# GpSimd's sums and gate products in the up-projection stage moved to VectorE

## The chip, the cores and the metric

The kernel runs on one core of one Trainium2 chip. The metric is the device time of one execution in microseconds (us). Three runs of the kernel before took 2186.55, 2191.22 and 2193.07 us; the median, 2191.22 us, is the time before.

## The reference

One block of a hybrid model, all in float32: 2048 tokens of width 1024, and a context of 256 tokens that gives only the starting state. What matters here is its second half, the feed-forward layer:

```
x = x + g1 * mix_x
x = x + g2 * swiglu(modulate(rmsnorm(x, norm2), sh2, sc2), w_up, w_down)
return rmsnorm(x, norm_f)

def swiglu(h, w_up, w_down):
    u = h @ w_up                      # 1024 -> 2 * 2816
    g, a = split(u, 2)
    return (silu(g) * a) @ w_down     # 2816 -> 1024
```

`g2` is a gate of 1024 numbers. Since it scales the columns of the layer's output, it can be multiplied into the columns of `w_down`.

## The kernel before

Every large product is done in two ways at once. First, a matrix is split into two halves in each direction, and seven products of half-size blocks, with sums of blocks as operands, stand in for eight (a scheme of Strassen's kind). Second, each float32 operand is split into a high and a low part, and each block product is three matmuls: high by high, high by low, low by high. ScalarE makes the high part (a cast, L146), VectorE the low part by subtraction (L149). A matmul has 128 rows and 512 columns.

The program has three long stages. From the start to about 840 us stand the projections, the scans of the mixer and the second norm. The **up-projection** runs from about 868 to 1760 us, in two halves of the tokens with 22 units each. The **down-projection** follows to the end. In the up-projection one unit is seven block products of 12 matmuls each (`product`, L586 to L588), 84 in all, which are named here by their right operand, h0 to h6, in program order. Their left operands come from two `raw` tiles of `w_up` (L633): the two for h0 and h1 are split as they are (`vt`), the others from block sums `ws` (L560) into `wh` and `wl`. The products h0, h2, h4 and h6 of a unit use one PSUM tile `pa`, h3 and h5 use `pg`, and h1 uses `pb`. Products h2, h4 and h6 add to what is in `pa`. After h4 VectorE reads `pa` into `a1` (L1266), and h6 may write `pa` only after that read. There are three `raw` buffers, and a unit needs two, so the loads for the next unit wait for the block sums of this one.

After every second unit `act_sums` forms four sums of blocks of the layer's activations (`small`, L1204) and stores seven blocks to HBM. In the second half of the tokens `w_sums` runs once per two units as well: it loads two 128x1024 tiles `big` of `w_down`, multiplies each half by the gate (L1230, four instructions), forms four differences (L1204) and stores seven blocks. The gate comes in a tile `adacc`. The sums go through four buffers `adaw`, each of which must have been stored before it is written again. At the start of the stage `last_norm` forms four differences (L1176). All of these, 180 instructions of 128x512, are on GpSimd (POOL).

The order on each engine is not the order of the text: a scheduler sets it from its own estimate of when each operand will be ready, and each engine then runs its list in that order. The loads and stores named here are issued by SyncE (SP), which also keeps to its list: a store whose source is not ready holds up the loads behind it.

Of the kernel before, what the change touches and what calls it, by code (L numbers as in the profile page):

```python
# [12 lines left out]
ALU = mybir.AluOpType  # L13
# [8 lines left out]
def tile_hybrid_block(ctx: ExitStack, tc: tile.TileContext, x, c, cx, c_ctx, w_ada, b_ada, norm1, w_in, conv_qk,  # L22
                      gate_bias, pool_w, pool_scale, head_norm, w_out, norm2, w_up, w_down, norm_f, out):
    nc = tc.nc
# [15 lines left out]
    def pool(name, bufs=1, side="left"):  # L40
        return tc.tile_pool(name=name, bufs=bufs, side=side, reuse_waits="tile")

    def psum(name, bufs):
        return tc.tile_pool(name=name, bufs=bufs, space=PSUM, reuse_waits="tile")
# [236 lines left out]
    def turn(psp, name, xs, d0, d1, a, b):  # L281

        for k0 in range(0, KD, 2):
            pt = psp.tile([P, 512], F32, name=name)
            for kk in range(2):
                for e in range(2):
                    o = kk * 256 + e * P
                    nc.tensor.transpose(out=pt[:, o:o + P], in_=xs[e][:, (k0 + kk) * P:(k0 + kk + 1) * P],
                                        identity=ident)
            for kk in range(2):  # L290
                k = k0 + kk
                src = pt[:, kk * 256:(kk + 1) * 256].rearrange("p (e c) -> p e c", e=2)
                dst = d0[:, :, k] if k < 4 else d1[:, :, k - 4]
                if kk:
                    nc.vector.tensor_scalar(dst, src, a[:, k:k + 1], b[:, k:k + 1], op0=ALU.mult, op1=ALU.add)
                else:
                    nc.scalar.activation(dst, src, AF.Identity, bias=b[:, k:k + 1], scale=a[:, k:k + 1])
            yield
# [58 lines left out]
    with pool("adap", 4, "right") as ap_:  # L357
        xc, turned = None, None
        for g in range(4):
# [39 lines left out]
            def col(o):  # L399
# [3 lines left out]
                                    op=ALU.add)  # L403
# [119 lines left out]
    def load_B(src, j, stp, name, bufs=3):  # L523

        t = b_tile(j)
        for k in range(4):
            st = stp.tile([P, 512], F32, name=name if isinstance(name, str) else name[k % 2], bufs=bufs)
            nc.scalar.dma_start(st, src[:, ORDER[j], k])
            split(st, t[:, 0, k], t[:, 1, k], nc.scalar, nc.vector)
        Btile[j] = t  # L530
# [94 lines left out]
    def load_raws(srcs, other=None):  # L625
        raws = []
        for src in srcs:
            if other is not None and raws:
                st = other.tile([P, KD, P], F32, name="rawx")
            else:  # L630
                st = rwp.tile([P, KD, P], F32, name="raw")
            with tc.issue_after(n_last.ins):
                raw_last[0] = nc.sync.dma_start(st, src.rearrange("(k p) c -> p k c", p=P))  # L633
            raws.append(st)
        return raws
# [141 lines left out]
    for half in range(2):  # L777
# [5 lines left out]
        if half == 0:  # L783
# [7 lines left out]
            def fin():  # L791
                fins.pop()(tp, "tp")
# [333 lines left out]
    def up_cols(f):  # L1126
        return [w_up[:, o + f * P:o + (f + 1) * P] for o in (0, DFF)]
# [35 lines left out]
    def last_norm(pair, xs):  # L1163

        half, i = divmod(pair, 4)
        yield
        d0 = last_x[0].rearrange("p (e k c) -> p e k c", e=2, k=4)
        d1 = xl.tile([P, 2, 4, P], F32, name="big")
        with tc.issue_after(mm_last[0].ins):
            for _ in turn(pmp, "pm", xs, d0, d1, A2, B2):  # L1170
                pass
        dst = s_hb[half][:, :, :, i * P:(i + 1) * P]

        def diff(a, b):
            t = adr.tile([P, 4, P], F32, name="adaw", bufs=4)
            nc.gpsimd.tensor_tensor(t, a, b, op=ALU.subtract)  # L1176
            return t
        t1 = diff(d0[:, 1], d0[:, 0])
        t2 = diff(d1[:, 1], t1)
        for b, t in ((0, d0[:, 0]), (1, d1[:, 0]), (2, d1[:, 1]), (3, t1), (4, t2), (5, diff(d1[:, 1], d0[:, 1])),  # L1180
                     (6, diff(d1[:, 0], t2))):
            nc.sync.dma_start(dst[:, b], t)
        yield
# [6 lines left out]
    with ExitStack() as pr:  # L1190
        wp = pr.enter_context(pool("m_w", 1))
        up_wp[0] = wp
        fin = None
        tmp = pr.enter_context(pool("m_a", 1))
        adr = pr.enter_context(pool("m_ad", 1))
        pup = pr.enter_context(psum("pup2", 2))

        def store(i, m, half, src):

            (nc.scalar if half and m == NM - 1 else nc.sync).dma_start(s_act[i, m, :, half], src)  # L1200

        def small(a, b, op):
            t = adr.tile([P, 512], F32, name="adaw", bufs=4)
            nc.gpsimd.tensor_tensor(t, a, b, op=op)  # L1204
            return t

        def act_sums(m, half, A11, A21, A12, A22):

            store(0, m, half, A11)
            store(1, m, half, A12)  # L1210
            store(6, m, half, A22)
            s1 = small(A21, A22, ALU.add)
            store(3, m, half, s1)
            s2 = small(s1, A11, ALU.subtract)
            store(4, m, half, s2)
            store(5, m, half, small(A11, A21, ALU.subtract))
            store(2, m, half, small(A12, s2, ALU.subtract))

        def w_sums(m):

            w1, w2 = (xl.tile([P, D], F32, name="big") for _ in range(2))
            with tc.issue_after(raw_last[0].ins):
                nc.sync.dma_start(w1, w_down[m * P:(m + 1) * P])
                nc.sync.dma_start(w2, w_down[(NM + m) * P:(NM + m + 1) * P])
            lo, hi = slice(0, 512), slice(512, 1024)
            for n in (lo, hi):
                g2r = adr.tile([P, 544], F32, name="adacc")[:, 0:512]
                nc.sync.dma_start(g2r, s_g[3:4, n].to_broadcast([P, 512]))
                for w in (w1, w2):
                    nc.gpsimd.tensor_tensor(w[:, n], w[:, n], g2r, op=ALU.mult)  # L1230
            nc.sync.dma_start(s_t[0, m], w1[:, lo])
            nc.sync.dma_start(s_t[1, m], w2[:, lo])
            nc.sync.dma_start(s_t[2, m], w2[:, hi])
            t1 = small(w1[:, hi], w1[:, lo], ALU.subtract)
            nc.sync.dma_start(s_t[3, m], t1)
            t2 = small(w2[:, hi], t1, ALU.subtract)
            nc.sync.dma_start(s_t[4, m], t2)
            nc.sync.dma_start(s_t[5, m], small(w2[:, hi], w1[:, hi], ALU.subtract))
            nc.sync.dma_start(s_t[6, m], small(w2[:, lo], t2, ALU.subtract))

        for half in range(2):
            if half:
                Btile = [None] * 7
            acts = []
            for ff in range(NF):
                m, fh = divmod(ff, 2)
                f = fh * NM + m
                first = half == 0 and f == 0
                make = up0 if first else operands(load_raws(up_cols(f)), up_wp)
                A = A0 if first else {}  # L1250
                for j, i in enumerate(ORDER):
                    if i not in A:
                        A[i] = make(i)
                    if Btile[j] is None:
                        load_B(s_hb[half], j, wp, "hst")
                g = [tmp.tile([P, 512], F32, name=f"g{n}", bufs=2) for n in range(2)]
                a1 = tmp.tile([P, 512], F32, name="a1")

                def sink(r, n, ps, sb):
                    if r == 0:  # L1260
                        nc.vector.tensor_tensor(g[n], ps, sb, op=ALU.add)  # L1261
                        nc.scalar.activation(g[n], g[n], AF.Silu)  # L1262
                        if n == 1:
                            nc.vector.tensor_tensor(g[1], g[1], a1, op=ALU.mult)  # L1264
                    elif n == 1:
                        nc.vector.tensor_tensor(a1, ps, sb, op=ALU.add)  # L1266
                    else:
                        nc.vector.tensor_tensor(g[0], g[0], ps, op=ALU.mult)
                norm = last_norm(order[-1] // 2, [X_.pop(m_) for m_ in (NCH - 1, NCH - 2)]) if first else iter(())
                for _ in unit(A, pup, tmp, sink):  # L1270
                    next(norm, None)
                acts += g
                if fin:
                    fin(pup, "pb", bufs=1)
                    fin = None
                if half == 0 and ff in (8, 12):
                    fin = ada_acc(5, (ff - 8) // 4, adr, 4)
                if fh:
                    act_sums(m, half, *acts)
                    acts = []  # L1280
                elif half == 1:
                    w_sums(m)
# [211 lines left out]
```

## Time and profile before

| | |
|---|---|
| median of three runs | 2191.22 us |
| the profiled execution | 2189.12 us |
| its span, first to last instruction | 2187.2 us |
| TensorE busy in the span | 2041.8 us (93%) |
| VectorE busy | 1442.3 us (66%) |
| ScalarE busy | 913.6 us (42%) |
| GpSimd busy | 508.9 us (23%) |
| mean granted TensorE clock | 0.971 |

Busy time is a sum over the whole span, so a stage must be read by itself: windows give busy times of one stretch, and the lists of waits say what ended the idle time of an engine there.

### The profile page before, as it was taken

The page shows a single profiled execution, that of the slowest core. Times are in us where ns is not written, and L with a number is a line of the kernel's source. Part 1 is how long each engine was busy: PE and PEld are TensorE (multiplying, and loading weights), DVE is VectorE, ACT ScalarE, POOL GpSimd, SP SyncE. Part 2 cuts the span into 40 slices and gives each one's busy share as a digit, 9 for nine tenths or more (in the row PEclk, how much of TensorE's full clock was granted, in tenths as well). Part 3 has the DMA queues.
Part 4 walks back from the last instruction along what each step waited for, and adds up shares of the span by engine and source line. Part 5 has one row for each costly group of instructions (what it writes and reads, how often), then busy time and mean ns, then how long its engine had stood idle before and what let it go on. Part 6 is the DMA issues. An engine that isn't in the chain of part 4 may idle for free.

```text
span 2187.2 us, 27588 instructions
## 1 busy us (share of the span) xinstructions
PE 2041.8 (93%) x9482; PEld 1647.5 (75%) x9482; DVE 1442.3 (66%) x2240; ACT 913.6 (42%) x1817; POOL 508.9 (23%) x402
## 2 busy tenths in 40 slices
PE   7998888996788998999999999999999999999998
PEld 3997666675677776888888877777777788888887
DVE  6876779888455566765665577766767664446664
ACT  5653654355343544533333344333323344433442
POOL 1000012310333322111121134435435311004121
PEclk9999999996899999999999999999999999999999
DMA  8697556468567765534342366545555594644642
GB/s 271 207 286 230 174 164 194 139 189 221 145 194 227 232 214 180 156 103 150 96 146 93 95 222 215 177 164 186 180 168 178 186 328 151 221 144 144 227 174 101
DMA packets 357267, 397.80 MB, mean 182 GB/s; under 512 B 22292, under 2 KB 243064, under 8 KB 357128
## 3 DMA queue, kind: packets, MB, share of 16 engines
q1 hardware_dynamic: 307728, 318.33, 45.9%
q10 hardware_dynamic: 49400, 77.73, 11.0%
q8 instruction: 74, 1.21, 0.2%
q14 instruction: 65, 0.53, 0.1%
HBM read 269.44 MB, written 126.54 MB: 181 GB/s over the span
## 4 chain that ended last, share of the span: by engine, by line
PE 45%; DMA 11%; DVE 8%; issue 7%; POOL 5%; ACT 2%; SPq 2%; ACTq 0%; POOLq 0%; DVEq 0%
PE pdn L1320 6%; PE pdn L1321 6%; PE pdn L1322 6%; PE pa L586 4%; PE pa L588 4%; PE pa L587 4%; PE pg L587 2%; PE pg L586 2%; PE pg L588 2%; DMA big<-in_w_down_dram 2%; POOL adaw L1204 2%; POOL big L1230 2%; DMA wb<-s_W 2%; DVE wl L149 1%; DMA raw<-in_w_up_dram 1%
## 5 line engine op out<-in xcount | busy, mean ns | idle before, releaser
L586 PE MATMUL pa<-h,wh 128*128 128x512 f32 x680 | 276.4, 409 | 28.3 <-DVE a L1266 18.0
L587 PE MATMUL pa<-h,wh 128*128 128x512 f32 x680 | 273.4, 403 | 1.5 <-DVE h L149 1.5
L588 PE MATMUL pa<-h,wl 128*128 128x512 f32 x680 | 271.8, 401 | 0.0
L1321 PE MATMUL pdn<-ow,op 128*128 128x512 f32 x616 | 239.0, 389 | 0.0
L1320 PE MATMUL pdn<-ow,op 128*128 128x512 f32 x616 | 238.0, 389 | 1.0 <-ACT op L146 1.0
L1322 PE MATMUL pdn<-ow,op 128*128 128x512 f32 x616 | 238.2, 389 | 0.0
L149 DVE TENSOR_TENSOR wl<-ws,wh 128x512 fp32r<-128x512 f32 x224 | 191.5, 862 | 58.8 <-ACT wh L146 58.1
L149 DVE TENSOR_TENSOR op<-ra,op 128x512 fp32r<-128x512 f32 x154 | 123.6, 809 | 157.0 <-ACT op L146 156.8
L146 ACT CAST wh<-ws 128x512 fp32r<-128x512 f32 x224 | 137.5, 618 | 193.2 <-PE pg L587 84.3
L146 ACT CAST op<-ra 128x512 fp32r<-128x512 f32 x154 | 95.1, 620 | 222.1 <-PE pdn L1322 219.4
L586 PEld LDWEIGHTS pa<-h,wh 128*128 128x128 f32 x680 | 131.0, 193 | 70.4 <-DVE a L1266 24.6
L1204 POOL TENSOR_TENSOR adaw<-g,g 128x512 f32<-128x512 f32 x44 | 66.2, 1504 | 502.0 <-DVE g L1264 502.0
L586 PE MATMUL pg<-h,wh 128*128 128x512 f32 x448 | 178.5, 399 | 2.9 <-ACT p L611 2.0
L587 PE MATMUL pg<-h,wh 128*128 128x512 f32 x448 | 177.5, 396 | 1.5 <-DVE h L149 1.4
L588 PE MATMUL pg<-h,wl 128*128 128x512 f32 x448 | 176.9, 395 | 0.0
L587 PEld LDWEIGHTS pa<-h,wh 128*128 128x128 f32 x680 | 131.1, 193 | 33.7 <-DVE h L149 2.6
L588 PEld LDWEIGHTS pa<-h,wl 128*128 128x128 f32 x680 | 130.4, 192 | 31.5 <-issue 0.7
L560 DVE TENSOR_TENSOR ws<-raw 128x512 f32<-128x512 f32 x110 | 79.4, 722 | 108.0 <-DMA raw<-in_w_up_dram 98.1
L1262 ACT ACTIVATE g<-g 128x512 f32<-128x512 f32 x88 | 55.7, 633 | 225.8 <-DVE g L1261 221.5
L149 DVE TENSOR_TENSOR vt<-raw,vt 128x512 fp32r<-128x512 f32 x108 | 105.2, 975 | 62.8 <-ACT vt L146 57.2
L1320 PEld LDWEIGHTS pdn<-ow,op 128*128 128x128 f32 x616 | 115.5, 188 | 25.3 <-ACT op L146 1.4
L1322 PEld LDWEIGHTS pdn<-ow,op 128*128 128x128 f32 x616 | 115.6, 188 | 24.1
(353 smaller groups left out, 4619.9 us busy)
## 6 DMA issues: line engine op xcount, KB each, us to landing
raw<-in_w_up_dram SPq DMA_DIRECT2D x88, 512.0 KB, 4.3
ra<-s_act SPq DMA_DIRECT2D x66, 512.0 KB, 6.0
s_act<-adaw SPq DMA_DIRECT2D x84, 256.0 KB, 2.6
rwt<-s_t SPq DMA_DIRECT2D x77, 256.0 KB, 3.5
adaw<-in_w_ada_dram SPq DMA_DIRECT2D x64, 256.0 KB, 3.1
s_act<-g SPq DMA_DIRECT2D x63, 256.0 KB, 2.8
s_ha<-hb SPq DMA_DIRECT2D x8, 1792.0 KB
hst<-s_ha ACTq DMA_DIRECT2D x56, 256.0 KB, 3.2
```

What stands on the lines that cost most here:

```text
L146: nc.scalar.copy(hi, src)
L149: eng_lo.tensor_tensor(lo, src, r32(hi), op=ALU.subtract)
L560: nc.vector.tensor_tensor(t, a, b, op=op)
L586: nc.tensor.matmul(ps, lhsT=ah[:, k], rhs=B[:, 0, k], start=st, stop=False, **kw)
L587: nc.tensor.matmul(ps, lhsT=ah[:, k], rhs=B[:, 1, k], start=False, stop=False, **kw)
L588: mm_last[0] = nc.tensor.matmul(ps, lhsT=al[:, k], rhs=B[:, 0, k], start=False, stop=(k == 3), **kw)
L1204: nc.gpsimd.tensor_tensor(t, a, b, op=op)
L1230: nc.gpsimd.tensor_tensor(w[:, n], w[:, n], g2r, op=ALU.mult)
L1262: nc.scalar.activation(g[n], g[n], AF.Silu)
L1320: nc.tensor.matmul(ps, lhsT=A[:, 0, ts_], rhs=W[:, 0], start=start, stop=False)
L1321: nc.tensor.matmul(ps, lhsT=A[:, 0, ts_], rhs=W[:, 1], start=False, stop=False)
L1322: nc.tensor.matmul(ps, lhsT=A[:, 1, ts_], rhs=W[:, 0], start=False, stop=stop)
```

## The change

Three helpers use VectorE in place of GpSimd for the same instruction on the same operands: the differences of `last_norm` (4 instructions), `small` (132) and the gate products in `w_sums` (44). After it GpSimd has nothing to do between the start of the up-projection and the down-projection.

```diff
@@ last_norm @@
         def diff(a, b):
             t = adr.tile([P, 4, P], F32, name="adaw", bufs=4)
-            nc.gpsimd.tensor_tensor(t, a, b, op=ALU.subtract)
+            nc.vector.tensor_tensor(t, a, b, op=ALU.subtract)
             return t
@@ small @@
             t = adr.tile([P, 512], F32, name="adaw", bufs=4)
-            nc.gpsimd.tensor_tensor(t, a, b, op=op)
+            nc.vector.tensor_tensor(t, a, b, op=op)
             return t
@@ w_sums @@
                 for w in (w1, w2):
-                    nc.gpsimd.tensor_tensor(w[:, n], w[:, n], g2r, op=ALU.mult)
+                    nc.vector.tensor_tensor(w[:, n], w[:, n], g2r, op=ALU.mult)
```

The scheduler places the moved instructions among VectorE's own and orders the others anew. This is VectorE's list before, from the last result of one unit (`g_13411`) to the read of `pa` of the next (`a_13571`), in the middle of the second half:

```order
L1268 TENSOR_TENSOR g_13411<-g_13411,pa 128x512 [waits PE_49]
L149 TENSOR_TENSOR vt<-raw,vt 128x512 [waits PE_49,Activation_49]
L149 TENSOR_TENSOR wl<-raw,wh 128x512 [waits Activation_49]
L1261 TENSOR_TENSOR g_13569<-pb,p_13587 128x512 [waits DMAHW2_49,Pool_49]
L149 TENSOR_TENSOR wl<-ws,wh 128x512 [waits PE_49,Activation_49] x2
L560 TENSOR_TENSOR ws<-raw,ws 128x512 [waits DVE_49]
L149 TENSOR_TENSOR vt<-raw,vt 128x512 [waits DMAHW3_49,PE_49,Activation_49]
L560 TENSOR_TENSOR ws<-raw 128x512 [waits DMAHW0_49,DVE_49]
L1266 TENSOR_TENSOR a_13571<-pa,p_13629 128x512 [waits PE_49]
```

The read of `pa` stands behind one instruction that waits for a load, the block sum of `raw`. The same stretch of VectorE's list after the change has the eight sums in its first part, of which the last four are shown with what stands around them:

```order
L1204 TENSOR_TENSOR adaw<-big 128x512 [waits DMAHW0_49]
L1261 TENSOR_TENSOR g_13569<-pb,p_13587 128x512 [waits DMAHW4_49,DVE_49]
L1204 TENSOR_TENSOR adaw<-big,adaw 128x512 [waits DMAHW2_49,DVE_49]
L149 TENSOR_TENSOR wl<-ws,wh 128x512 [waits PE_49,Activation_49]
L1204 TENSOR_TENSOR adaw<-big 128x512 [waits DMAHW3_49]
L1204 TENSOR_TENSOR adaw<-big,adaw 128x512 [waits DMAHW4_49,DVE_49]
L149 TENSOR_TENSOR wl<-ws,wh 128x512 [waits PE_49,Activation_49]
L560 TENSOR_TENSOR ws<-raw,ws 128x512 [waits DVE_49]
```

Here the sums wait for stores (`DMAHW`), and the block sum that frees a `raw` buffer, the last row, stands behind all eight of them. Then follow, still on VectorE after the change, the rows up to the read of `pa`:

```order
L149 TENSOR_TENSOR vt<-raw,vt 128x512 [waits DMAHW1_49,PE_49,Activation_49]
L560 TENSOR_TENSOR ws<-raw 128x512 [waits DMAHW1_49,DVE_49]
L1261 TENSOR_TENSOR g_13570<-pg,u_13615 128x512 [waits DMAHW6_49,PE_49]
L149 TENSOR_TENSOR wl<-ws,wh 128x512 [waits Activation_49]
L1230 TENSOR_TENSOR big<-big,adacc 128x512 [waits DMAHW2_49]
L560 TENSOR_TENSOR ws<-ws,raw 128x512 [waits DVE_49]
L1230 TENSOR_TENSOR big<-big,adacc 128x512 [waits DMAHW3_49]
L1266 TENSOR_TENSOR a_13571<-pa,p_13629 128x512 [waits PE_49]
```

The read of `pa` now stands behind three instructions that wait for loads: the block sum of `raw` and two gate products. On SP, the list before had the load of `raw` and the two of `w_down` between the stores of the sums:

```order
L1237 DMA s_t<-adaw 128x512 [waits DMAHW2_49,Pool_49]
L1238 DMA s_t<-adaw 128x512 [waits DMAHW3_49,Pool_49]
L633 DMA raw<-in_w_up_dram 128x8x128 [waits DMAHW4_49,DVE_49]
L1223 DMA big<-in_w_down_dram 128x1024 [waits DMAHW5_49]
L1239 DMA s_t<-adaw 128x512 [waits DMAHW6_49,Pool_49]
L1224 DMA big<-in_w_down_dram 128x1024 [waits DMAHW7_49]
```

After the change SP has the three loads in one block behind the last store:

```order
L1238 DMA s_t<-adaw 128x512 [waits DMAHW3_49,DVE_49]
L1239 DMA s_t<-adaw 128x512 [waits DMAHW4_49,DVE_49]
L633 DMA raw<-in_w_up_dram 128x8x128 [waits DMAHW5_49,DVE_49,Activation_49]
L1223 DMA big<-in_w_down_dram 128x1024 [waits DMAHW6_49]
L1224 DMA big<-in_w_down_dram 128x1024 [waits DMAHW7_49]
```

## Rows read from the trace of the kernel before

**Rows 1.** Windows of the stages: us, busy us (instructions) per engine, granted clock, DMA.

```profile
core 0: us, PE busy (x) PEld busy (x) DVE busy (x) ACT busy (x) POOL busy (x), PEclk, DMA share, GB/s
868.00:1302.00 434.00, 429.96 (x1837) 346.10 (x1837) 278.75 (x398) 166.79 (x290) 69.03 (x47) 1.00 0.42 133
1302.00:1360.00 58.00, 52.87 (x212) 39.96 (x212) 49.83 (x58) 26.84 (x48) 31.75 (x19) 0.97 0.68 226
1360.00:1760.00 400.00, 381.18 (x1610) 303.37 (x1608) 271.84 (x302) 124.00 (x225) 172.75 (x112) 0.99 0.54 178
1760.00:2187.00 427.00, 419.21 (x1848) 346.77 (x1848) 235.47 (x335) 164.09 (x310) 63.88 (x31) 1.00 0.53 186
```

**Rows 2.** Waits, 1302 to 1760 us: us in total, times, longest us.

```profile
POOL big L1230 <- DMA big<-in_w_down_dram: 57.0, 11, 8.1
...
DVE ws L560 <- DMA raw<-in_w_up_dram: 55.8, 19, 5.8
...
PE pa L586 <- DVE a L1266: 18.0, 15, 3.7
```

**Rows 3.** Windows of shorter stretches, columns as in rows 1.

```profile
1000.00:1100.00 100.00, 100.00 (x431) 80.72 (x430) 62.33 (x93) 35.98 (x63) 11.58 (x8) 1.00 0.36 113
1302.00:1336.00 34.00, 29.73 (x116) 22.07 (x116) 32.49 (x38) 17.82 (x32) 18.90 (x11) 0.95 0.79 263
1400.00:1440.00 40.00, 36.34 (x151) 29.06 (x150) 25.94 (x31) 11.46 (x21) 16.65 (x12) 0.96 0.52 174
1480.00:1520.00 40.00, 37.48 (x155) 29.87 (x154) 27.36 (x32) 13.28 (x24) 14.66 (x11) 0.96 0.54 165
```

**Rows 4.** Timeline of TensorE: start, us, instruction, idle before and what ended it.

```profile
871.70 0.50 PE L588 MATMUL pa<-h,vt 128*128 128x512 f32 x1 [2.00 <-DVE vt L149]
...
1412.87 0.80 PE L586 MATMUL pa<-h,wh 128*128 128x512 f32 x1 [3.66 <-DVE a L1266]
```

**Rows 5.** Timeline of VectorE, 1388 to 1422 us, columns as in rows 4.

```profile
1399.44 1.67 DVE L560 TENSOR_TENSOR ws<-raw,ws 128x512 f32<-128x512 f32 x1
1401.03 1.78 DVE L149 TENSOR_TENSOR vt<-raw,vt 128x512 fp32r<-128x512 f32 x1
1408.64 0.69 DVE L560 TENSOR_TENSOR ws<-raw 128x512 f32<-128x512 f32 x1 [5.83 <-DMA raw<-in_w_up_dram]
1409.25 0.68 DVE L1261 TENSOR_TENSOR g<-pg,u 128x512 f32<-128x512 f32 x1
...
1412.13 0.68 DVE L1266 TENSOR_TENSOR a<-pa,p 128x512 f32<-128x512 f32 x1
```

**Rows 6.** Timeline of SP's queue, 1350 to 1765 us: start and us of each issue.

```profile
1403.99 0.32 SPq L1239 DMA_DIRECT2D s_t<-adaw  x1
1404.41 0.38 SPq L633 DMA_DIRECT2D raw<-in_w_up_dram  x1
1404.85 0.68 SPq L1223 DMA_DIRECT2D big<-in_w_down_dram  x1
1405.58 0.42 SPq L1224 DMA_DIRECT2D big<-in_w_down_dram  x1
```

**Rows 7.** Timeline of GpSimd, 1388 to 1422 us, columns as in rows 4.

```profile
1402.23 1.74 POOL L1204 TENSOR_TENSOR adaw<-big,adaw 128x512 f32<-128x512 f32 x1
1409.89 3.45 POOL L1230 TENSOR_TENSOR big<-big,adacc 128x512 f32<-128x512 f32 x2 [5.93 <-DMA big<-in_w_down_dram]
1416.77 2.99 POOL L1230 TENSOR_TENSOR big<-big,adacc 128x512 f32<-128x512 f32 x2 [3.42 <-DMA adacc<-s_g]
```

**Rows 8.** Groups of VectorE, 1302 to 1760 us: busy us, mean ns, idle before.

```profile
L149 DVE TENSOR_TENSOR wl<-ws,wh 128x512 fp32r<-128x512 f32 x85 | 93.8, 1118 | 11.5 <-ACT wh L146 11.4
...
L1264 DVE TENSOR_TENSOR g<-g,a 128x512 f32<-128x512 f32 x23 | 15.7, 684 | 0.8 <-ACT g L1262 0.7
```

**Rows 9.** Timeline of ScalarE, 1396 to 1416 us, columns as in rows 4.

```profile
1400.89 0.62 ACT L146 CAST wh<-ws 128x512 fp32r<-128x512 f32 x1 [1.17 <-PE pg L587]
```

**Rows 10.** Loads of `raw` by line L633, 1340 to 1760 us: time to landing.

```profile
DMA to landing us min/median/max: 4.6/6.2/6.7
```

## The prediction

> **What bounds the kernel now.** I read the windows of the stages first, then the waits, then the timelines of one place. In [rows 1] the reader is to see that TensorE is busy for 430 of 434 us in the first half of the up-projection and for 419.2 of 427 us in the down-projection, so nothing but TensorE's own work counts there. The second half of the up-projection is different: 52.9 of 58 us and 381.2 of 400 us. Of the four windows these are also the two where GpSimd is busy for over 40% of the time. What TensorE waits for there stands in the list of waits [rows 2]: 18.0 us in 15 waits of h6 for VectorE's read of `pa` (L1266). VectorE itself waits 55.8 us for loads of `raw`, more than for anything else that this stage shows on it.
>
> The timelines show one such place, the longest wait of the kind, 3.66 us [rows 4]. VectorE ends the block sum that frees a `raw` buffer at 1401.1 and then sits for 5.83 us until the next `raw` lands at 1408.6; the read of `pa` comes at 1412.13, four instructions later [rows 5]. The load was short, 4.2 us from its issue at 1404.41 [rows 6]. It was issued 3.3 us late, because SP stood on the store of GpSimd's last sum, which ran from 1402.23 to 1403.97 [rows 6, 7]. So two things feed the wait: slow sums that hold up SP, and VectorE's own delay.
>
> That delay is visible too. A VectorE instruction of 128x512 takes 0.68 to 0.69 us and the next starts 0.60 us after it [rows 5]. With both operands in SBUF and GpSimd at work it takes 1.67 or 1.78 us [rows 5], and the 85 `wl` subtractions average 1.118 us where a like instruction, L1264, takes 0.684 [rows 8]. That is 85 x 0.434 = 37 us lost in this stage on one group alone. The Trainium skill, "SBUF — State Buffer", section "Who interferes with whom", says that the two engines share one pair of ports by an exclusive lock and that the loser waits for the whole instruction. The trace agrees as far as its direction goes: VectorE's instruction is longer by 1.0 to 1.1 us, a little less than a whole GpSimd instruction beside it. By that rule each pair of overlapping instructions would cost VectorE more than doing both itself, which is also what the rows give.
>
> **The change part by part.** In the second half 131 instructions leave GpSimd [rows 1], 19 and 112 in its two windows, and VectorE gets them at 0.60 us each, 79 us in 458. Against this stand at least the 37 us of `wl`, and as much again if the other groups of SBUF operands suffer as `wl` does. I take VectorE's load as unchanged, 272 + 50 us of 458, 70%. What changes is what stands in whose way.
>
> *The steady part, 1360 to 1760 us.* I follow one period of two units, 168 matmuls, 39.0 us at 100/431 = 0.232 us each [rows 3]. It begins, for this purpose, at Z, when h2 of the first unit ends and frees a `wl` buffer. In TensorE's new order 61 matmuls, 14.2 us, stand between Z and h6 of the same unit. Within this time VectorE must get to L1266. The cast on ScalarE takes 0.62 us [rows 9]; with 0.3 us for signals, my estimate, the `wl` row runs at Z+0.9. Behind it stand two sums, a `wl` and the block sum that frees a `raw` buffer, so that one ends at Z+0.9+4x0.60+0.69 = Z+4.0. The stores that the sums wait for were issued before, so I take no wait there. SP now has the stores of all sums behind it and issues `raw` at once. With 4.2 us it lands at Z+8.2. The block sum, `g` and `wl` take it to Z+10.0. The first gate product needs the first `w_down` tile: issued 0.44 us behind `raw` and used 5.0 us after its issue [rows 6, 7], so Z+9.5, no wait. The second tile is issued 1.2 us behind `raw`. GpSimd's two products of 3.45 us started at 1409.89, so the second began by 1411.6, 6.0 us after that tile's issue [rows 6, 7]; that gives Z+11.2. VectorE reaches it at Z+11.2 too. L1266 then ends near Z+12.5. TensorE wants it at Z+14.2: 1.7 us to spare, where the kernel before was late by 1.8 us per period on average, 18.0 us in ten. If `raw` takes the longest of [rows 10], 6.7 us, and the tiles of `w_down` with it 2.5 us more, L1266 ends at Z+15.0 and h6 waits 0.8 us. The third gate product needs a gate that is loaded once the second has freed `adacc`; GpSimd waited 3.42 us for it [rows 7], five of VectorE's instructions, 3.0 us, fill that time, and nothing that TensorE wants within 5 us is queued behind it. In the other unit of the period the read of `pa` stands ahead of the block sum that waits for `raw`, so no load is in its way, and 24 matmuls, 5.6 us, lie between h4 and h6.
>
> The first end of this term is all 18.0 us of L1266's waits. I leave 0.3 us per period in ten periods and take -15 us. The other end is that VectorE's list is late as often as now: 0.
>
> *The clock.* In the three windows of [rows 3] with waits of TensorE the granted clock is 0.95 and 0.96, that is, for a part of them the lower level, 1.2 GHz, in place of 2.4 GHz; before it fell TensorE had stood idle in each, 3.66 us at 1412. At half speed the missing share is lost work: 40 x 0.04 = 1.6 us in each of the two later ones, 34 x 0.05 = 1.7 us in the first. If the waits go, so do these. I take -3 us for the two later ones (0 to -3.2).
>
> *The switch of halves, 1302 to 1360 us.* TensorE idles 5.1 of 58 us here, and more than that with the clock. VectorE is the reason: 32.5 busy us of 34 [rows 3], since it also makes the split operands of the new half. Of its 38 instructions most should shrink to 0.60 us, and 11 come from GpSimd: 49 x 0.60 = 29.4 us. That is 3 us less work, but the gate products now stand in this row with loads that share the DMA engines (share 0.79) with the new half's. I take -2 us, from -6 to +5.
>
> *The start of the stage.* TensorE waits 2.0 us for a `vt` at 871.70 [rows 4], which VectorE made beside GpSimd's four differences. The one difference that now stands ahead of that `vt` costs 0.6 us, and the overlap that made neighbours 1 us longer each is gone. I take -1.5 us, from -2 to +3.
>
> *The first half.* 44 sums, 26 us more on VectorE beside 279 of 434 us, hidden behind a TensorE that never waits; the read of `pa` keeps 23 matmuls, 5.3 us, of room, as before. 0, up to +2 if that cover fails at some units. *The hand-over to the down-projection.* The last sums stand ahead of the first operands there: two or three, 1.2 to 1.8 us on a path that now has overlap of the same size. 0, from -1 to +2.
>
> Sum: -15 - 3 - 2 - 1.5 = -21.5 us against the profiled execution's 2189.1 us, whose span is 2187.2 us, gives 2167.6. That execution was 2.1 us below the median of the three runs, so I forecast **2170 us** for the median.
>
> **Rivals.** *The loads become VectorE's.* Before, GpSimd sat 57.0 us waiting for `w_down` [rows 2], at no cost, as nobody stood behind it; now VectorE's whole list stands behind the gate products, and L1266 right behind the second. It decides from the point where that tile lands over 13 us after Z, 7.7 us after its issue in place of 6.0: each microsecond beyond costs TensorE one per period. To eat the whole gain it must take 2 us more, near 10 us from issue; at 12 us the ten periods lose 10 x 4.3 = 43 us against a gain of 21.5, and the time is 2191 + 21 = about 2212 us. For it: three loads of 512 KB now leave SP in one block, and [rows 10] reaches 6.7 us. Against it: the place shown left SP in just this block and landed in 4.2 to 6.0 us [rows 6, 7]. Milder cases of this kind end at 2198 to 2212. Chance 0.12.
>
> *The waits only move.* VectorE's load is as before, and its list is one list. If its row of eight sums waits for the four `adaw` buffers, which empty only when their stores have landed, the block sum that frees `raw` comes later by as much. At 1.7 us of such waits per period nothing is to spare, at 4 us the L1266 waits are as long as now. Then the terms of the steady part and of the clock vanish, those of the switch and the start remain or turn: 2185 to 2194 us, say 2188. For it: GpSimd needed 1.3 to 1.7 us per sum [rows 7] and so gave each store time to land, VectorE needs 0.6. Against it: five of VectorE's own instructions stand between those sums. Chance 0.18.
>
> *Everything goes.* All waits of L1266, the clock's 4.9 us and most of the switch's idle time: 2191 - 18 - 4.9 - 5 - 2 = 2161 us. Chance 0.15; my forecast has 0.55.
>
> **How the numbers follow.** A change below 0.3%, 6.6 us, can't be told from none here. My forecast's own range is 2164 to 2183; it and the case in which everything goes are faster, 0.70. The moved waits lie mostly within 0.3% (2184.6 to 2197.8): 0.17 with the mildest late loads. Slower: 0.13. The range that leaves 2 in 10 out runs from 2159, the bounds at their best ends, to 2195, where the moved waits end; beyond it lie the late loads and a little at the bottom.
>
> **What would show it.** Right: no VectorE instruction of 128x512 above 0.7 us in the up-projection; h6's wait for L1266 below 3 us in all after 1360; 39 to 39.5 us per period there; clock 1.00 in the windows of [rows 3] but the first; SP issuing `raw` within 0.3 us of the block sum that frees it; waits for `w_down` and `adacc` on VectorE, with TensorE unmoved. Wrong, by the first rival: gate products ended by loads, and L1266 and h6 late behind them. Wrong, by the second: VectorE idle before sums until stores land. A gain that lies in the first half or the down-projection would refute the working, whatever the total.

## The result, and the profile after

The changed kernel takes 2154.57 us, the median of four runs (2148.61 to 2162.95), against 2188.89 us for four runs of the kernel before on the same chip: a ratio of 0.9849, 95% interval 0.9826 to 0.9873. Four later runs of it gave 2156.88 us and 0.9853 (0.9830 to 0.9877). It is faster by some 33 us. I had forecast 2170 us and a range from 2159 to 2195, so the sign was right, the forecast gain of 21 us was a third too small, and the time lies below the range. Set on the 2191.22 us from which I forecast, the ratio gives 2158.1 us (2153.1 to 2163.4), only just below it.

These are windows of the profiled execution after, cut so that they hold the work of [rows 1]:

```profile
core 0: us, PE busy (x) PEld busy (x) DVE busy (x) ACT busy (x) POOL busy (x), PEclk, DMA share, GB/s
859.00:1293.00 434.00, 429.45 (x1838) 344.74 (x1836) 286.30 (x450) 169.50 (x294) 0.00 (x0) 1.00 0.42 134
1293.00:1346.00 53.00, 50.50 (x212) 39.51 (x213) 44.90 (x73) 24.81 (x46) 0.00 (x0) 1.00 0.77 252
1346.00:1720.00 374.00, 373.03 (x1608) 302.16 (x1607) 257.90 (x409) 128.93 (x227) 0.00 (x0) 1.00 0.57 189
1720.00:2146.00 426.00, 418.98 (x1848) 346.68 (x1847) 233.37 (x338) 163.65 (x309) 60.00 (x28) 1.00 0.53 186
```

The counts of matmuls make this a ledger. The first half of the up-projection does 1837 or 1838 matmuls in 434 us in both kernels. The switch of halves does 212 in 53 us where it took 58. The steady part does 1608 in 374 us, where 1610 took 400. The down-projection is the same but for what lies outside the rounded cuts, 0.4 us. That is -31 us, all between 1302 and 1760 us of the old time. VectorE has more instructions than in [rows 1], 409 against 302 in the steady part, and is busy for less time, 258 against 272 us.

The profiled spans differ by more, 40.4 us (2187.2 and 2146.8). The other 9.3 us lie before the stage, which began at 858.63 and not at 867.96, behind engine lists that are the same up to there. I count them as scatter between executions: both profiled executions of the changed kernel were the fastest of their four, and the profiled runs below whose edits lie in the up-projection alone begin it anywhere from 857.67 (e7) to 871.72 us (e6). The 2 or 3 us that the medians gain beyond the 31 are not explained.

VectorE's groups after, 1293 to 1720 us, as in [rows 8]:

```profile
L149 DVE TENSOR_TENSOR wl<-ws,wh 128x512 fp32r<-128x512 f32 x84 | 57.4, 684 | 9.3 <-ACT wh L146 9.2
...
L1230 DVE TENSOR_TENSOR big<-big,adacc 128x512 f32<-128x512 f32 x40 | 26.6, 687 | 6.2 <-DMA adacc<-s_g 5.2 <-DMA big<-in_w_down_dram 1.0
...
L1204 DVE TENSOR_TENSOR adaw<-big,adaw 128x512 f32<-128x512 f32 x22 | 15.1, 688 | 9.9 <-DMA s_act<-adaw 9.9
```

The `wl` subtractions are back from 1118 to 684 ns each. In the waits of the same stretch TensorE no longer appears for L1266; the relation has turned round [rows 2]:

```profile
DVE ws L560 <- DMA raw<-in_w_up_dram: 49.7, 19, 3.7
DVE a L1266 <- PE pa L588: 14.7, 10, 4.7
...
DVE adaw L1204 <- DMA s_act<-adaw: 11.4, 9, 3.0
...
DVE big L1230 <- DMA adacc<-s_g: 5.2, 9, 2.0
```

VectorE now waits 14.7 us for TensorE to finish `pa`, so it is early. It still waits as often for `raw`, and for stores and gates as well, and TensorE loses nothing by it. One period, SyncE first, then VectorE [rows 5, 6]:

```profile
1537.58 0.38 SPq L633 DMA_DIRECT2D raw<-in_w_up_dram  x1
1538.02 0.57 SPq L1223 DMA_DIRECT2D big<-in_w_down_dram  x1
```

```profile
1536.82 0.69 DVE L560 TENSOR_TENSOR ws<-raw,ws 128x512 f32<-128x512 f32 x1
...
1541.62 0.69 DVE L560 TENSOR_TENSOR ws<-raw 128x512 f32<-128x512 f32 x1 [2.67 <-DMA raw<-in_w_up_dram]
...
1544.63 0.68 DVE L1230 TENSOR_TENSOR big<-big,adacc 128x512 f32<-128x512 f32 x1
1545.23 0.68 DVE L1266 TENSOR_TENSOR a<-pa,p 128x512 f32<-128x512 f32 x1
```

The block sum ends at 1537.51, `raw` is issued 0.07 us later, and the read of `pa` comes 3.6 us after `raw` is there, as I had laid it out.

### The profile page after: what moved, and what is told of

It is laid out like the page before. It is cut to its first block, busy times and chain, and to the rows that moved or that the text cites. A ratio compares the mean times of both kernels' runs of the same rounds, so it can differ in the third digit from the quotient of the medians.

```text
span 2146.8 us, 27478 instructions
## 1 busy us (share of the span) xinstructions
PE 2026.7 (94%) x9482; PEld 1643.8 (77%) x9482; DVE 1426.9 (66%) x2420; ACT 918.9 (43%) x1817; POOL 227.9 (11%) x222
## 4 chain that ended last, share of the span: by engine, by line
PE 63%; DMA 7%; DVE 5%; ACT 1%; issue 1%; POOL 1%; SPq 0%; ACTq 0%; POOLq 0%; DVEq 0%
PE pa L586 7%; PE pa L588 7%; PE pa L587 7%; PE pdn L1320 7%; PE pdn L1322 7%; PE pdn L1321 6%; PE pg L588 3%; PE pg L586 3%; PE pg L587 3%; PE pm L1104 2%; PE pm L1102 2%; PE pm L1103 2%; PE pb L588 2%; PE pb L586 2%; PE pb L587 2%; DMA hst<-s_hb 2%
## 5 line engine op out<-in xcount | busy, mean ns | idle before, releaser
L586 PE MATMUL pa<-h,wh 128*128 128x512 f32 x680 | 273.0, 403 | 11.1 <-ACT p L600 6.6
L587 PE MATMUL pa<-h,wh 128*128 128x512 f32 x680 | 270.6, 399 | 0.0
L149 DVE TENSOR_TENSOR wl<-ws,wh 128x512 fp32r<-128x512 f32 x224 | 155.6, 697 | 54.7 <-ACT wh L146 53.8
L1352 POOL TENSOR_TENSOR hr<-hr,o 128x1024 f32<-128x1024 f32 x8 | 21.7, 2733 | 1098.1 <-ACT o L1365 928.4
L1320 PEld LDWEIGHTS pdn<-ow,op 128*128 128x128 f32 x616 | 115.6, 188 | 25.2 <-ACT op L146 1.4
L1322 PEld LDWEIGHTS pdn<-ow,op 128*128 128x128 f32 x616 | 115.6, 188 | 24.1
L1321 PEld LDWEIGHTS pdn<-ow,op 128*128 128x128 f32 x616 | 115.7, 188 | 23.9
L1102 PE MATMUL pm<-h,mh 128*128 128x512 f32 x256 | 106.7, 417 | 3.5 <-ACT mh L146 2.9
```

The costliest lines, as they stand in the source:

```text
L149: eng_lo.tensor_tensor(lo, src, r32(hi), op=ALU.subtract)
L586: nc.tensor.matmul(ps, lhsT=ah[:, k], rhs=B[:, 0, k], start=st, stop=False, **kw)
L587: nc.tensor.matmul(ps, lhsT=ah[:, k], rhs=B[:, 1, k], start=False, stop=False, **kw)
L1102: nc.tensor.matmul(pt, lhsT=mh[:, k], rhs=w[:, 0, k % 4], start=(k == 0), stop=False)
L1320: nc.tensor.matmul(ps, lhsT=A[:, 0, ts_], rhs=W[:, 0], start=start, stop=False)
L1321: nc.tensor.matmul(ps, lhsT=A[:, 0, ts_], rhs=W[:, 1], start=False, stop=False)
```

## The experiments

Two theories stood against each other. **Ports**: GpSimd's instructions beside VectorE's lengthen these, and VectorE's late list is what TensorE waits for. **Queue**: GpSimd's slow sums hold SyncE at their stores, and the loads of `raw` behind them come late.

All runs stand in one table. The spans are read from the timeline of VectorE, between the starts of its product `g<-g,a` (L1264) in the 20th, 30th and 44th unit; the last column is the time from there to the down-projection's first matmul. One profiled execution each; medians and ratios are over all runs, each against runs of the kernel before beside it.

| kernel | median us | ratio (95%) | units 20-30 | units 30-44 | to down-pr. |
|---|---|---|---|---|---|
| before | 2182.9 to 2188.9 | 1 | 217.8 | 283.9 | 2.3 |
| after | 2154.57 | 0.9849 (0.9826-0.9873) | 200.8 | 269.6 | 2.3 |
| after_again | 2156.88 | 0.9853 (0.9830-0.9877) | 201.0 | 269.6 | 2.3 |
| e1_sums | 2171.63 | 0.9948 (0.9928-0.9967) | 209.7 | 278.2 | 2.3 |
| e2_gates | 2178.27 | 0.9969 (0.9949-0.9989) | 213.1 | 280.0 | 2.3 |
| e3_ghost | 2197.15 | 1.0055 (1.0028-1.0082) | 216.9 | 280.1 | 11.6 |
| e4_own | 2209.26 | 1.0123 (1.0096-1.0149) | 230.2 | 289.2 | 2.3 |
| e5_half2 | 2159.38 | 0.9885 (0.9846-0.9924) | 205.4 | 269.6 | 2.3 |
| e6_fill | 2167.61 | 0.9925 (0.9891-0.9960) | 201.5 | 269.6 | 14.1 |
| e7_hold | 2193.42 | 1.0047 (1.0028-1.0067) | 219.0 | 270.0 | 22.8 |
| e8_ghost_mid | 2180.45 | 0.9966 (0.9949-0.9982) | 213.9 | 280.3 | 2.3 |
| e9_hold_mid | 2172.03 | 0.9925 (0.9895-0.9955) | 216.1 | 271.5 | 2.3 |
| e10_ghost_late | 2172.64 | 0.9943 (0.9915-0.9971) | 206.5 | 280.6 | 2.3 |
| c1_mixer | 2165.11 | 0.9921 (0.9893-0.9949) | 202.1 | 269.6 | 2.3 |

### Sums alone, gates alone (e1_sums, e2_gates)

```diff
@@ e1: small @@
-            nc.gpsimd.tensor_tensor(t, a, b, op=op)
+            nc.vector.tensor_tensor(t, a, b, op=op)
@@ e2: w_sums @@
-                    nc.gpsimd.tensor_tensor(w[:, n], w[:, n], g2r, op=ALU.mult)
+                    nc.vector.tensor_tensor(w[:, n], w[:, n], g2r, op=ALU.mult)
```

> Only the 132 sums of `small` go to VectorE; the 44 gate products and the 4 differences of last_norm stay on GpSimd. Ports theory (the loss was VectorE made slow by GpSimd beside it): about a third of the overlap, that of the gate products, stays, so 18 to 25 us faster than before, 2164 to 2171 us, with VectorE instructions of 1.6 us beside the gate products only. Queue theory (the loss was SP held up by GpSimd's slow sums, so that `raw` was issued late): SP is as free as with the whole change, so about 30 us faster, 2157 to 2161 us.

> Only the 44 gate products go to VectorE; the sums stay on GpSimd. Ports theory: a third of the overlap goes, 8 to 14 us faster, 2175 to 2181 us. Queue theory: SP still stands on the stores of slow sums, 0 to 4 us faster, 2185 to 2189 us. If the gate products' loads become VectorE's waits and nothing else is won: slower by up to 10 us.

Sums alone gain 0.5%, some 11 us, and gates alone 0.3%, some 7. The times came within 1 us of Ports' ranges, but the kernel before took 2184.68 us beside them: as gains, 11 and 7 us fall short of the 18 to 25 and 8 to 14 that Ports expected. e1 missed Queue's 2157 to 2161 by over 10 us, and e2 gained more than Queue's 0 to 4. That is no clean test of Queue, though, since SyncE is not free in e1, as its expectation had it: in units 30 to 44 one load of `raw` per period still leaves 2.1 to 3.8 us after the subtraction that frees its buffer, behind the store of a gate product (L1233). The two gains add up to 18 us, where the whole change gains 33. So what either leaves on GpSimd costs most of what all of it costs.

### Overlap put back (e3_ghost, e8_ghost_mid, e10_ghost_late)

The whole change, and after each moved sum or gate product GpSimd adds its first 384 columns to themselves, into a buffer that nobody reads. VectorE's and SyncE's work is that of the changed kernel.

```diff
@@ e3: small, and the same line in w_sums @@
             nc.vector.tensor_tensor(t, a, b, op=op)
+            nc.gpsimd.tensor_tensor(gh, t[:, 0:384], t[:, 0:384], op=ALU.add)
@@ e8: at is half and m of the units at hand @@
+            if not (at[0] and at[1] == NM - 1):
+                nc.gpsimd.tensor_tensor(gh, t[:, 0:384], t[:, 0:384], op=ALU.add)
@@ e10 @@
+            if at[0] and 2 <= at[1] < NM - 1:
+                nc.gpsimd.tensor_tensor(gh, t[:, 0:384], t[:, 0:384], op=ALU.add)
```

> The whole change, and beside it GpSimd adds, after each moved instruction, the first 384 columns of its result to themselves into a tile that nobody reads: GpSimd as busy as before by three quarters, VectorE's and SP's lists in the steady part as after the change, no store and no operand behind GpSimd. The only new waits are those for a buffer to be written again. Ports theory: VectorE's instructions beside GpSimd take 1.4 us and more again, and 12 to 30 of the 33 us are lost: 2167 to 2185 us. Queue theory: within 5 us of the changed kernel, 2152 to 2160 us.

> As the ghost run (whole change, and GpSimd adds 384 columns of each moved result to themselves, into a dead buffer), but without the ghosts of the last pair of units of the second half, whose buffer held back the down-projection's first loads by 10.2 us in that run. Theory Ports, with overlap as the cost of the old kernel's steady part: unit 26 to 44 takes 363-368 us (346.2 after the change, 367.9 before), the switch (unit 20 to 26) 128-133 us, and the time is 2178-2190. Theory Queue: SyncE is not held here, so 2153-2165.

> The ghosts of e8 only in the second half from its third pair of units on, without the last pair. If the steady part's loss is overlap alone, and doesn't come from a late start that the switch hands on: the switch 124-126 us as after the change, unit 26 to 44 363-367, the time 2168-2178. If the steady waits are a delay handed on from the switch (it fills buffers late, and nothing catches up): unit 26 to 44 within 5 us of the changed kernel's 346, 2153-2162.

In e3 the ghosts took the whole gain, but not all of that is overlap: the dead buffer lies where the down-projection's first loads go, so these waited for the last ghost, and the last column shows 9.3 us for it. e8 leaves out the last ghosts, and the column is back at 2.3. VectorE's groups of e8, 1400 to 1700 us, and what TensorE waits for there (L1276 is that kernel's L1266):

```profile
L149 DVE TENSOR_TENSOR wl<-ws,wh 128x512 fp32r<-128x512 f32 x60 | 50.6, 851 | 1.3 <-ACT wh L146 1.3
L149 DVE TENSOR_TENSOR vt<-raw,vt 128x512 fp32r<-128x512 f32 x29 | 33.7, 1161 | 0.0
```

```profile
PE pa L586 <- DVE a L1276: 12.6, 8, 3.0
```

The long instructions and the waits for L1266 are back, with `raw` issued within 0.07 us of the end of VectorE's last read before it (seven places from 1404 to 1464 us in e3), and in e8 VectorE never waits for GpSimd between 1300 and 1760 us. So overlap alone, with additions three quarters as long as the old ones, costs 10.7 of the 14.3 us between units 30 and 44. In e10, whose ghosts begin some units into the second half, it costs the same 11.0 us there, and only 5.7 us before, 0.8 of them ahead of unit 26. The steady part's loss is therefore made in each period, and not handed on from the switch. Ports' numbers held for e8; e10's total did and its units 26 to 44, 362.1 us, fell just short of 363; e3 came out above its 2185, by 3 us if the held loads are taken off. Queue's ranges, 2152 to 2165 in all, failed in e3 and e8.

### Fills in place of additions (e6_fill)

```diff
@@ in the places of e3's addition @@
+            nc.gpsimd.tensor_copy(gh[:, 0:2], t[:, 0:2])
+            for _ in range(3):
+                nc.gpsimd.memset(gh, 0.0)
```

> The whole change, and after each moved sum and gate GpSimd waits for it, copies two columns and then fills a dead buffer three times (384 columns each), as long as the ghost addition of the earlier run or about as long (1.1-1.3 us), but without reading operands. Theory Ports in the form 'GpSimd and VectorE share a way to SBUF that GpSimd's two-operand instructions hold': fills leave VectorE's instructions at 0.69 us and the time at 2150-2162. If any GpSimd instruction of that length beside VectorE slows it: VectorE instructions above 1 us and 2180-2200, as with the ghost additions. If it was the added waits for VectorE's results and for buffers that cost, not the overlap: 2180-2200 with VectorE's instructions at 0.69.

GpSimd is as busy in the same places, and VectorE doesn't notice it. GpSimd's fills and VectorE's `wl` of e6, 1400 to 1700 us:

```profile
L1207 POOL MEMSET tokq<- 128x384 f32 x271 | 113.8, 420 | 15.7
```

```profile
L149 DVE TENSOR_TENSOR wl<-ws,wh 128x512 fp32r<-128x512 f32 x62 | 42.4, 684 | 7.3 <-ACT wh L146 7.3
```

Units 30 to 44 take 269.6 us, to a tenth the changed kernel's time. The median, 2167.61, is above it by the loads held at the end, as in e3, 14.1 - 2.3 = 11.8 us; without them it would be 2156, within Ports' range, which the median missed. So the added waits and the third engine cost nothing, and what costs is that GpSimd reads operands beside VectorE. The Trainium skill, "SBUF — State Buffer", section "Who interferes with whom", says just this: a VectorE instruction with two SBUF inputs contends with a GpSimd instruction that reads SBUF and not with one that only writes. The runs agree: 851 ns beside additions, 684 ns beside fills.

### The hold of SyncE (e4_own, e7_hold, e9_hold_mid)

e4 is the kernel before with the stores of GpSimd's eight sums issued by GpSimd, which takes the hold away. e7 is the whole change with the hold put back: a first piece of each sum's store, 128 of 512 columns, comes from a buffer that GpSimd fills ten times, so zeros take the place of a quarter of each sum. e9 leaves the last pair of units out.

```diff
@@ e4: the stores of the eight sums (condensed) @@
-            nc.sync.dma_start(s_act[i, m, :, half], src)
+            nc.gpsimd.dma_start(s_act[i, m, :, half], src)
@@ e7, e9: the same eight stores (condensed; k is the filled buffer) @@
+            nc.gpsimd.tensor_copy(k[:, 0:2], t[:, 0:2])
+            for _ in range(10):
+                nc.gpsimd.memset(k, 0.0)
+            nc.sync.dma_start(dst[:, 0:128], k)
-            nc.sync.dma_start(dst, t)
+            nc.sync.dma_start(dst[:, 128:512], t[:, 128:512])
```

> The kernel before, with the stores of GpSimd's sums (eight per two units) issued by GpSimd itself in place of SP, so that no load of `raw` or w_down stands behind a sum on SP; the overlap of GpSimd and VectorE stays. Ports theory: no more than 5 us faster, 2184 us or above. Queue theory: 15 to 25 us faster, 2164 to 2174 us.

> The whole change, but each of the eight sums of a unit pair is stored in two pieces, and the first piece (128 of 512 columns, zeros, so a quarter of each stored sum is left out) comes from a buffer that GpSimd first fills ten times, some 1.3-1.6 us after VectorE's sum. So SyncE's queue is held by slow stores as before the change, and operand loads issue behind them, while GpSimd reads no operands beside VectorE. Theory Queue: the wait for L1266 comes back, 2175-2192. Theory Ports: the hold alone costs little, 2152-2165. If both are needed (a late load only hurts when the block sum is late too): 2160-2175.

> As the hold run (first quarter of each sum's store, zeros, waits for ten fills of GpSimd), but not in the last pair of units of the second half, where the fills held back the down-projection's first loads by 21.4 us. What is left is the hold of SyncE's queue alone: with the stage of that run, 18-20 us above the changed kernel, nearly all of it in the switch and the three units behind it (135 against 124 us to unit 26, then 8): 2170-2178. If the hold mattered in the steady part too, unit 30 to 44 takes over 272 us.

e4 is slower than the kernel before by 1.2%, which by the letter is Ports' "2184 us or above" and not Queue's 2164 to 2174. In its trace `raw` leaves 0.03 us after the read that frees it, so the hold is gone, but the overlap is not the old one. The VectorE instruction that ran longest in one period, and GpSimd's work beside it:

```profile
1533.69 6.62 DVE L149 TENSOR_TENSOR wl<-raw,wh 128x512 fp32r<-128x512 f32 x1
```

```profile
1534.12 1.31 POOL L1204 TENSOR_TENSOR adaw<-adaw,g 128x512 f32<-128x512 f32 x1
1535.37 1.30 POOL L1204 TENSOR_TENSOR adaw<-g,g 128x512 f32<-128x512 f32 x1
1536.61 0.56 POOL L1208 DMA_DIRECT2D s_act<-adaw  x1
1537.20 1.31 POOL L1204 TENSOR_TENSOR adaw<-g,adaw 128x512 f32<-128x512 f32 x1
1538.46 1.29 POOL L1204 TENSOR_TENSOR adaw<-big 128x512 f32<-128x512 f32 x1
1539.69 1.11 POOL L1208 DMA_DIRECT2D s_act<-adaw  x2
```

One VectorE instruction of 0.69 us stands through a whole series of four sums and a store. In the kernel before no single one in the up-projection took over 1.8 us. e4 therefore says nothing on Queue by its total.

e9 says more, with VectorE's instructions at 0.684 us (62 `wl`); its 2172.03 us lie in the expected range. A hold is there: one load of `raw` per period leaves 1.6 to 2.2 us after the block sum that frees its buffer in units 30 to 44, and VectorE waits longer for `raw`, 67.8 us in 15 waits between 1400 and 1700 us, against 37.8 in 15 after the change.

```profile
DVE ws L560 <- DMA raw<-in_w_up_dram: 67.8, 15, 6.6
```

Yet units 30 to 44 take 271.5 us, 1.9 more than after the change, so this hold alone is nearly absorbed. It is not the hold of the kernel before, however. There, in units 30 to 44, the load behind the last sum leaves at once (0.02 or 0.03 us), and two others in each period leave late, by 1.6 us behind a sum's store and by 2.0 to 3.7 us behind a gate product's (L1233). No run puts these back alone.

The trace of the kernel before helps here. Of its 11 waits for L1266 in those units (12.7 us), 6 (7.5 us) stand behind the load that left at once, so a hold of that load is not what made them late. One of these is the second longest wait of the stage, 2.52 us:

```profile
1484.15 1.66 DVE L560 TENSOR_TENSOR ws<-raw,ws 128x512 f32<-128x512 f32 x1
...
1492.18 0.69 DVE L560 TENSOR_TENSOR ws<-raw 128x512 f32<-128x512 f32 x1 [4.67 <-DMA raw<-in_w_up_dram]
```

The block sum ends at 1485.81 and SyncE issues the load at 1485.84. The other 5 (5.2 us) stand behind a load issued right after the one that left 2.0 to 3.7 us late, and the ghosts of e8, which bring back a wait in each period at the first place, bring back none at the second. What the hold adds there is open.

In units 20 to 30 e9's hold is not absorbed: 216.1 us, nearly the 217.8 of the kernel before. But e8 without a hold has 213.9 there. Either cause alone costs 13 to 15 of the 17 us, so in the switch their shares in the old kernel can't be told apart; and e9's hold is not quite the old one, since it issues eight stores more per pair of units and comes to 2.2 to 3.8 us where the old one was 0.8 to 3.3. e7's total came out just above what Queue expected, but 20.5 us of it are loads held at the end, as in e3; without them it would be 2173, in the range for both causes being needed.

### The second half alone (e5_half2)

```diff
@@ up-projection, before small @@
+        eng = [nc.gpsimd]
@@ small @@
-            nc.vector.tensor_tensor(t, a, b, op=op)
+            eng[0].tensor_tensor(t, a, b, op=op)
@@ last_norm @@
-            nc.vector.tensor_tensor(t, a, b, op=ALU.subtract)
+            nc.gpsimd.tensor_tensor(t, a, b, op=ALU.subtract)
@@ loop over the halves @@
             if half:
+                eng[0] = nc.vector
```

> The change made in the second half of the stage alone: the sums of the first half and the differences t1..t6 of the residual stage stay on GpSimd, the sums of the second half and the gates go to VectorE. If all of the gain lies where gates, differences and sums come together (the traces of before and after show unit 20 at 391.4 and 391.7 us from the stage's start, so nothing in the first half): 2150-2160 us, as the whole change. If the first half and the start give 1.5 us or more, as I predicted, and the clock too: 2158-2165. If GpSimd's presence earlier shifts the switch of the halves: above 2165.

The median, 2159.38 us, lies in both of the first two ranges and doesn't choose between them. The interval, 0.9846 to 0.9924, holds the whole change's ratio. The steady part is the same to a tenth; units 20 to 30 take 4.6 us more, and GpSimd is still busy for 6.5 us between 1300 and 1400 us, with sums of the first half.

### Carried on into the mixer (c1_mixer)

```diff
@@ ml_a @@
-        nc.gpsimd.tensor_tensor(X, X, mask[:, :, None, :].to_broadcast([P, 2, 4, P]), op=ALU.add)
-        nc.gpsimd.tensor_tensor(wb, wb, qd, op=ALU.mult)
+        nc.vector.tensor_tensor(X, X, mask[:, :, None, :].to_broadcast([P, 2, 4, P]), op=ALU.add)
+        nc.vector.tensor_tensor(wb, wb, qd, op=ALU.mult)
@@ low parts mlo @@
-        split(pm, mh[:, 0:4], mlo[:, 0:4], nc.scalar, nc.vector if cc == order[0] else nc.gpsimd)
+        split(pm, mh[:, 0:4], mlo[:, 0:4], nc.scalar, nc.vector)
```

> The change carried on into the stages before the up-projection: GpSimd's mask addition (2.45 us, 16 times), its product wb (1.35 us, 16 times) and its low parts mlo (1.29 us, 15 times) of the mixer also on VectorE, where they should take 1.2, 0.69 and 0.69 us. Theory Ports: VectorE's neighbours get back to 0.69 and 1.2 us and TensorE's waits for raw L1030 (13.7 us in three places) shrink: 2138-2152. Rival: VectorE's queue is the bound there (its share is 59% from 600 to 840 us, and the new work is waited for in order): 2155-2170.

The time came out as the rival had it: 2165.11 us, and 0.9921 against 0.9849, with intervals that don't meet, a loss of 8 to 15 us by medians or ratios. From unit 20 on c1 is as fast as after the change, within 1.3 us up to unit 44, so the loss should lie before. VectorE's waits of c1, 600 to 870 us, show two that were GpSimd's, and TensorE's show more behind VectorE than after the change:

```profile
DVE raw L1023 <- DMA raw<-s_R: 14.7, 9, 3.9
...
DVE wb L1024 <- DMA wb<-s_W: 10.5, 7, 2.7
```

```profile
PE pm L1102 <- DVE hb L295: 7.9, 3, 3.8
...
PE pm L1086 <- DVE h L1067: 4.1, 4, 2.2
```

After the change these were 0.6 us for L1102, and L1086 did not wait for L1067 at all. Instructions did get shorter, L1067 from 1183 to 690 ns, but the waits for `raw` and `wb`, which were GpSimd's, now stand in VectorE's list. That they are the loss is not shown: e10, whose mixer is unchanged, has 3.0 us at L1102 and 3.2 us at L1086 behind L1067, and began its up-projection at 871.38 us, later than c1 at 869.73.

### The changed kernel again (after_again)

> The changed kernel once more, beside the others: 2150-2162. It shows how far the stages before the up-projection differ between executions of one program: if its up-projection starts within 1 us of 858.6, the 9.3 us by which that stage began earlier than before the change are the change's, through the order of the instructions; if it starts anywhere between 855 and 870, they are scatter.

Its median is in the expected range, and its up-projection began at 858.76 us, 0.13 us from the first profile, so by the letter of the expectation the early start would be the change's. The other runs say otherwise: with edits in the up-projection alone, e3, e6, e8, e9 and e10 began it between 866.65 and 871.72 us and e7 at 857.67, where the kernel before began it at 867.96. The early start is scatter.

## Why the prediction was right in sign and wrong in size

**What held.** The gain lies where TensorE waited for L1266; the first half and the down-projection gave nothing; VectorE's load did not grow; the steady part runs at 39.0 us per period (from unit 30 to unit 42); and the waits that moved to VectorE (11.4 us for stores, 5.2 and 1.0 for gate and `w_down`) leave TensorE alone. The granted clock is 1.00 in the windows of [rows 3] that I named, and in the first one too:

```profile
1293.00:1327.00 34.00, 32.74 (x137) 25.41 (x138) 27.69 (x45) 17.46 (x32) 0.00 (x0) 1.00 0.81 263
1400.00:1440.00 40.00, 40.00 (x174) 32.45 (x173) 28.12 (x45) 13.72 (x24) 0.00 (x0) 1.00 0.63 205
1480.00:1520.00 40.00, 40.00 (x174) 32.40 (x174) 28.24 (x46) 13.62 (x24) 0.00 (x0) 1.00 0.58 186
```

**The terms.**

| term | forecast us | measured us |
|---|---|---|
| start and first half | -1.5 | 0 |
| switch of halves | -2 | -5 |
| steady part and its clock | -15 - 3 | -26 |
| hand-over | 0 | 0 |
| sum | -21.5 | -31 |

**The step that failed is the bound of the steady part**, "The first end of this term is all 18.0 us of L1266's waits". That was no bound, because a row's idle time is not what a wait costs. TensorE's timeline of the kernel before, at the second longest such wait, shows it:

```profile
1490.62 0.40 PE L586 MATMUL pa<-h,wh 128*128 128x512 f32 x1
1493.53 0.50 PE L586 MATMUL pa<-h,wh 128*128 128x512 f32 x1 [2.52 <-DVE a L1266]
1493.87 0.39 PE L587 MATMUL pa<-h,wh 128*128 128x512 f32 x1
...
1494.67 0.63 PE L587 MATMUL pa<-h,wh 128*128 128x512 f32 x1
1495.10 0.63 PE L588 MATMUL pa<-h,wl 128*128 128x512 f32 x1
```

At full rate starts lie 0.232 us apart. Here 2.91 us pass from start to start, so 2.68 are lost where the row says 2.52, since idle time counts from a modelled end. The next start comes 0.34 us later, and then some lie 0.43 apart; the granted clock from 1494.6 to 1496.5 us is 0.50, the lower level, 1.2 GHz. Summed over all starts from 1360 to 1760 us, the loss is 18.0 (idle rows) + 2.5 (extra at the 15 waits) + 3.5 (22 slow starts) + 1.6 (others) = 25.6 us. I had 15 + 3. What I left out is the 3 us that I kept as leftover waits, of which none came, the 2.5 and 1.6, which no idle row shows, and 0.5 of clock. The count of matmuls in [rows 1] would have said it at once: 1610 x 0.232 = 373.5 us of work in a window of 400.

**The switch** is the second mis-sized term. I took only VectorE's shorter work, 3 us, less a little for gate products behind loads. The gate products cost nothing, and 5 of the 58 us went, near the best end of my bounds, -6. **The start** gave nothing: from the stage's first matmul to the first read of `pa` are 22.3 us before and 22.0 after, and to unit 20's product 388.1 and 388.4 (391.5 in after_again).

**The rivals.** The case in which everything goes, to which I gave 0.15, is what happened, and its price of 2161 us was too high for the same reason as above. The lower end of my range has a slip besides: 2159 is the profiled execution's 2189.1 less the bounds' 30.2, without the 2.1 us that the forecast adds for the median; with them it is 2161. The late loads and the moved waits are both in the trace, on VectorE, without weight. **The cause.** I named two things that feed the wait, SyncE's hold and VectorE's long instructions, and the one place that I showed had both; it is of units 20 to 30, and in units 30 to 44 the load at that place isn't held. In units 30 to 44 the runs give the overlap 10.7 of 14.3 us, with additions three quarters as long; of the other 3.6 the hold's share is open. In units 20 to 30 the two can't be separated. Shares of the moved work misled, too, in the expectations of the runs: e1 leaves GpSimd 4 of its 12 instructions per period and e2 leaves it 8, and they won back only 5.7 and 3.9 of the 14.3 us.

## What to carry to other kernels

To size what can be won back from waits of the bounding engine, count its instructions in the stage and multiply by its full pace; the sum of its idle rows is too small. When two engines read SBUF side by side, try the whole of the slower one's two-operand work on the faster one before judging by a part, since a third of the overlap (e1) still cost 8.6 of 14.3 us here. Do it stage by stage: the same move in this kernel's mixer lost time.

## What was not expected of the hardware

A VectorE instruction beside GpSimd's sums is usually held for about one of them (1.67 to 1.78 us in all [rows 5]). Where GpSimd issues the sums' stores itself, a single one was held for 6.62 us, through four sums and the store between them, and this recurred (6.61 us at 1446.21 and at 1575.69). The Trainium skill, "SBUF — State Buffer", section "Who interferes with whom", says that issue order decides which engine blocks; the runs show that one side can win several times in a row. And 1.37 us of fills on GpSimd after each result (with the copies of two columns 144 of 300 us) left every group of VectorE's at 0.684 to 0.692 us.
